# Ten and eleven seven-product pairs in the right half of the down projection, and a stretched second attention half

## The chip, the cores and the metric

The kernel runs on one core of a Trainium2 chip. The metric is the device time of one execution in microseconds (us). Time before: 2152.0 us, the median of three runs (2150.22, 2152.0 and 2154.43). The profile is that of one further execution.

## The reference

Two layers (`DEPTH = 2`) of a decoder trunk over 256 tokens of width 2048, all in float32:

```python
for l in range(DEPTH):
    h = _rmsnorm(x, attn_norm_g[l])
    proj = h @ w_in[l]                       # 2048 x 6144
    q, k, v, gate_b, gate_c, conv_in = jnp.split(proj, splits, axis=-1)
    ...                                      # QK-norm; differential attention, 8 heads; sub-layer norm
    conv = gate_b * _short_conv(gate_c * conv_in, conv_w[l])
    x = x + jnp.concatenate([attn, conv], axis=-1) @ w_out[l]       # 2048 x 2048
    hm = _rmsnorm(x, mlp_norm_g[l]) @ w_up[l]                       # 2048 x 8192
    x = x + jnp.square(jax.nn.relu(hm)) @ w_down[l]                 # 8192 x 2048
```

## The kernel before, in words

**Products.** Every weight and every activation is split into a high part (rounded to `fp32r` by ScalarE, e.g. L302) and a low part (the rest, by VectorE, e.g. L303). A product is three matmuls: high by high, high by low, low by high (`TERMS`). Weights come by DMA on SyncE's queue (SP) into raw tiles (four buffers), are split into `whi` and `wlo` (three buffers each, pool `wpool`) and used once. `Weights.take` hands out the next split tile and has those of up to three more jobs issued ahead.

**Order.** The order of TensorE (PE) is written out by the program (`manual_schedule`). The order on the other engines and on the DMA queues is worked out by the framework's scheduler from its own estimate of times, so it can move when anything else does. Attention, norms and the like are Python generators run beside the large products: `work.tick()` is called after each few matmuls, and a piece goes on after as many ticks as it last yielded.

**Mixer, per layer.** Six products q, k, v for heads 0 to 3, then for heads 4 to 7 (`linear`); then gc and ci four times in turn (`linear_t`, 64 matmuls and 16 ticks each, names gc00, ci00, gc01 ... in layer 0 and gc10 ... in layer 1), gb four times, and the output projection. Attention for heads 0 to 3 starts 3 ticks after the first v and runs beside q, k, v of the second half (`pace` 1). Attention for heads 4 to 7 starts 9 ticks into gc (`pace` 2). In `attention` each head is a `unit`: scores `sc` on PE, max and bias on VectorE (L610), exp on ScalarE (L619), weighting on VectorE (L622 to L630), then, 10 ticks later, transposes `ptp` on PE (L635), their split `pT` (L637, L638), and 4 ticks later the product with v, `av` (L646). `staggered` starts the four units 8 ticks apart. After the last unit the result is normed (L661 to L671), and after a further 12 (pace 1) or 18 ticks (pace 2) transposed, `atp`, and split into `cat` (L677 to L684). Beside gc and ci, VectorE also splits four weight tiles for each `linear_t`, joins its result (L422) and runs the short convolution (L772, L696), and GpSimd (POOL) multiplies by the norm's factors (L769, L700).

**MLP, per layer.** 32 pairs of 256 hidden columns. Of each pair the hidden values are computed (L949), squared, and multiplied by the left half of w_down (columns 0 to 1023) by seven products of blocks in place of eight (L992), as in Strassen's method; hidden values are also stored in DRAM, with the four sums that the seven products need where the pair is in `SEVEN` (`hid7`, L979), else without (`hid`, L984). Then the right half of w_down (columns 1024 to 2047) is taken with the stored hidden values. First the last two pairs (30 and 31), which are still on the chip. Then pairs 0 to `2 * BLK` - 1 one at a time: those in `SEVEN` by seven products (21 matmuls of 128x512), the others by `ordinary` (24). A pair of seven products needs its w_down rows split in other forms (`quarters`, L834 to L869: VectorE L840, L853, L856, L857; ScalarE L839) and its hidden values split after loading (L1099, L1100); an ordinary one has two `whi`/`wlo` tiles. Seven-product pairs gather four of their products in PSUM banks of their own (`prods` 1, 5, 6, 7), which `seven_onto(2)` adds onto x at the end (L1055, L1047, L1063: one ScalarE and eight VectorE instructions). Then the remaining pairs, two together as a block: `columns` takes block b for 512 columns at a time, 48 matmuls for a block's two halves, in the hand-written `order`. Of the hidden values, a pair's or block's tile `fb` comes from pool `apool` (four buffers, shared with the next layer's normed tiles nT), the first block's from `fpool`.

With `BLK = 12` pairs 0 to 23 are taken singly, nine of them by seven products, in both layers, and blocks 12, 13 and 14 follow in the order (12,0), (13,0), (12,1), (14,0), (13,1), (14,1).

**Between layers.** While the last blocks run in layer 0, the next layer's norm is made in four chunks (`norm.chunk`: eight transposes on PE (L454) into two PSUM banks, ScalarE L270 and VectorE L271 from there, squares on ScalarE L472). Chunks 0 and 1 need x's left half, chunks 2 and 3 the two column groups as they come out. Beside this, SP loads the first weights of the next stage: in the mixer, the four 1 MB tiles `uraw` that the MLP starts with (L809) follow in SP's queue once the attention's buffers are free.

Of the kernel before, what the change touches and what calls it, by code (L numbers as in the profile page):

```python
# [10 lines left out]
F32R = mybir.dt.float32r  # L11
# [4 lines left out]
P = 128  # L16
# [19 lines left out]
NB2 = DFF // (KG * P)  # L36


SEVEN = (2, 4, 7, 9, 12, 14, 17, 19, 22)
BLK = 12  # L40

TERMS = ((0, 0), (0, 1), (1, 0))
REL = 2 * S - P - 1
# [45 lines left out]
def staggered(pieces, apart):  # L89

    entries = [[i * apart, p] for i, p in enumerate(pieces)]
    while entries:
        for e in list(entries):
            if e[0] <= 0:
                try:
                    e[0] = max(1, next(e[1]))
                except StopIteration:
                    entries.remove(e)
                    continue
            e[0] -= 1  # L100
        if entries:
            yield 1
# [3 lines left out]
def trunk(ctx: ExitStack, tc: tile.TileContext, x, w_in, w_out, conv_w, q_norm_g, k_norm_g,  # L106
# [6 lines left out]
    apool = ctx.enter_context(tc.tile_pool(name="apool", bufs=4))  # L113
# [12 lines left out]
    def bank(name):  # L126
        return ps.tile([P, CH], F32, tag="bank", name=name)

    def wide(name):
        return nat.tile([P, CH], F32, tag="wide", name=name)  # L130

    work = Background()
# [292 lines left out]
    def rstd_of(ss, n, name, shape):  # L425

        e = small.tile([P, shape], F32, tag="rs_e", name=f"{name}_e")
        nc.gpsimd.tensor_scalar(e, ss, 1.0 / n, EPS, op0=ALU.mult, op1=ALU.add)
        r = small.tile([P, shape], F32, tag="rs_r", name=f"{name}_r")
        nc.gpsimd.tensor_tensor(r, e, mhalf[:, :shape], op=ALU.pow)  # L430
        return r
# [152 lines left out]
    def attention(l, qT, kT, kL, v, h0, dst, bias, tmp, pace):  # L584
# [9 lines left out]
        def unit(i):  # L594
# [31 lines left out]
            for t in range(NT):  # L626
# [2 lines left out]
                                               nlam[:, l:l + 1], op0=ALU.mult, op1=ALU.mult)  # L629
                nc.vector.scalar_tensor_tensor(p[:, w], s[:, 1, w], c[:, t:t + 1], s[:, 0, w],  # L630
                                               op0=ALU.mult, op1=ALU.add)
            yield 10
            tp = bank(f"ptp{h}")
            for b in range(3):
                nc.tensor.transpose(tp[:, b * P:(b + 1) * P], p[:, b * P:(b + 1) * P], ident)  # L635
            pT = tmp.tile([P, 2, 3 * P], F32R, tag="pT", name=f"pT{h}", bufs=1)
            nc.scalar.activation(pT[:, 0], tp[:, :3 * P], AF.Copy)  # L637
            nc.vector.tensor_sub(pT[:, 1], tp[:, :3 * P], pT[:, 0].bitcast(F32))  # L638
            yield 4

            av = ps.tile([P, CH], F32, tag="av", name=f"av{h}", bufs=1)
            av = av.rearrange("p (t n c) -> p t n c", t=NT, n=2)
# [19 lines left out]
            f = rstd_of(flat, P, f"a{h0}", 4 * NT)  # L662
# [3 lines left out]
            for t in range(NT):  # L666
# [3 lines left out]
                    ao[:, t].rearrange("p (g d) -> p g d", d=P),  # L670
                    f2[:, :, t:t + 1].to_broadcast([P, 4, P]), op=ALU.mult)  # L671
                an_.append(an)
            yield 12 if pace == 1 else 18
            for t in range(NT):
                tp = bank(f"atp{h0}_{t}")
                for b in range(4):
# [7 lines left out]
                    op0=ALU.mult, op1=ALU.subtract)  # L684
                yield 2

        yield from staggered([unit(i) for i in range(4)], 8)
        dst.ready = True

    def conv(l, q, u, cv, norm):  # L690
# [99 lines left out]
    def mlp(l, mnorm, last):  # L790

        norm = None if last else Norm(0, l + 1)
        mT = mnorm.tiles
        with ExitStack() as scope:
            upool = scope.enter_context(tc.tile_pool(name="upool", bufs=4))
            fpool = scope.enter_context(tc.tile_pool(name="fpool", bufs=2))
# [34 lines left out]
            def quarters(i, col=0):  # L831


                keep = late if i == 0 or (i == SEVEN[0] and col) else lambda ins: None  # L834

# [55 lines left out]
            for i in range(NP - LAG, NP):  # L891
# [5 lines left out]

            order = [(b - n, n) for b in range(BLK, NB2) for n in range(2)
                     if BLK <= b - n < NB2 - 1]

# [12 lines left out]
            def blocks_of(order):  # L913
                for b, n in order:
                    box = []
                    four(b, n, 0, box)
                    four(b, n, 2, box)

            blocks_of([(NB2 - 1, 0), (NB2 - 1, 1)])
            for i in range(2 * BLK):  # L920
                if i in SEVEN:
                    weights.jobs += quarters(i, 2 * CH)
                    continue
                box = []
                for k in range(2):
# [5 lines left out]
            hid = {i: dram.tile([P, 2, 4 * P], F32R, name=f"hid{l}p{i}")  # L931
                   for i in range(NP - LAG) if i not in SEVEN}
            hid7 = {i: dram.tile([P, 8 * P], F32, name=f"hid{l}s{i}") for i in SEVEN}

# [27 lines left out]
            def square(i, h):  # L962
# [9 lines left out]
                if i < NP - LAG:  # L972
# [4 lines left out]
                    nc.vector.tensor_sub(h[:, S4], h[:, A12], h[:, S2])  # L977
                if i in SEVEN:
                    nc.gpsimd.dma_start(hid7[i], h.rearrange("p a c -> p (a c)"))  # L979
# [16 lines left out]
            for i in range(NP):  # L996
                j = i - LAG
                end = i == NP - 1
# [13 lines left out]
                for c in range(2):  # L1012
# [15 lines left out]
                    if j >= 0 and c == 0:  # L1028
                        b11, b21, b22 = weights.take()
                        t1, t3 = weights.take()  # L1030
                        f = fs[j]
# [5 lines left out]
                    elif j >= 0:  # L1037
                        t2, t4 = weights.take()
                        f = fs[j]
# [6 lines left out]
            def onto(dst, p, base):  # L1046
                nc.vector.scalar_tensor_tensor(dst, p, mnorm.scale, base,  # L1047
                                               op0=ALU.mult, op1=ALU.add)

            def seven_onto(n):  # L1050


                x11, x21, x12, x22 = (xs[n + i][:, t] for i in range(2) for t in range(NT))
                e1, e2, e3, e4 = wide("e1"), wide("e2"), wide("e3"), wide("e4")
                nc.scalar.activation(e1, prods[1], AF.Copy, scale=mnorm.scale)  # L1055
                onto(e2, prods[6], e1)
                onto(e4, prods[5], e2)
                onto(x22, prods[5], x22)
                onto(e3, prods[7], e2)

                def add():
                    for dst, v in ((x11, e1), (x12, e4), (x21, e3), (x22, e3)):
                        nc.vector.tensor_add(dst, dst, v)  # L1063

                return add
# [23 lines left out]
            def pair(i, f=None, at=0):  # L1089

                if f is None:
                    f = apool.tile([P, 2, 8, P], F32R, tag="a", name="fb")
                if i not in SEVEN:
                    nc.gpsimd.dma_start(
                        f[:, :, at:at + 4].rearrange("p a k c -> p a (k c)"), hid[i])
                    return f
                back = fpool.tile([P, 8, P], F32, tag="h", name="back", bufs=1)
                nc.gpsimd.dma_start(back.rearrange("p a c -> p (a c)"), hid7[i])
                nc.scalar.activation(f[:, 0], back, AF.Copy)  # L1099
                nc.vector.tensor_sub(f[:, 1], back, f[:, 0].bitcast(F32))  # L1100
                return f

            def block(b):

                pool, tag = (fpool, "f") if b == BLK else (apool, "a")
                f = pool.tile([P, 2, 8, P], F32R, tag=tag, name="fb")
                for j in range(2):
                    pair(2 * b + j, f, 4 * j)
                return f
# [15 lines left out]
            def by_token(f, n):  # L1125

                parts = [weights.take() for _ in range(KG // 2)]
                for t in range(NT):
                    for k in range(KG):
                        for m, (pa, pw) in enumerate(TERMS):  # L1130
                            nc.tensor.matmul(  # L1131
                                accs[n][:, t], f(k, pa, t), parts[k // 2][pw][:, k % 2],
                                start=False, stop=(k == KG - 1 and m == 2))
                        work.tick()

            def columns(f, n, start=False, stop=False):

                for kp in range(KG // 2):
                    hi, lo = weights.take()
                    for k in (2 * kp, 2 * kp + 1):  # L1140
                        for t in range(NT):
                            for m, (pa, pw) in enumerate(TERMS):
                                nc.tensor.matmul(  # L1143
                                    accs[n][:, t], f(k, pa, t), (hi, lo)[pw][:, k % 2],
                                    start=(start and k == 0 and m == 0),
                                    stop=(stop and k == KG - 1 and m == 2))
                        work.tick()

            fs = {30: fs[30], 31: fs[31], 0: pair(0)}
            for n in range(2):  # L1150
                columns(lambda k, pa, t: fs[NP - LAG + k // 2][:, pa, k % 2 * 2 + t], n, start=True)
            for i in range(2 * BLK):
                if i + 1 < 2 * BLK:
                    fs[i + 1] = pair(i + 1)
# [5 lines left out]
                start, end = i == SEVEN[0], i == SEVEN[-1]  # L1160
# [11 lines left out]
                    if n == 5:  # L1172
                        work.tick()
                work.tick()
            seven_onto(2)()
            if not last:
                work.start(norm.chunk(0, 2), 6)
                work.start(norm.chunk(1, 2), 11)

            for b, n in order:  # L1180
                if n == 0 and b + 1 < NB2 - 1:
                    blocks[b + 1] = block(b + 1)
                units = lambda k, pa, t, f=blocks[b]: f[:, pa, 2 * k + t]
                if last and (b, n) == order[-1]:
                    by_token(units, n)
                else:
                    columns(units, n, stop=(b == NB2 - 2))
                if b == NB2 - 2:
                    for t in range(NT):
                        onto(xs[2 + n][:, t], accs[n][:, t], xs[2 + n][:, t])  # L1190
                    if last:
                        store(2 + n)
                    else:
                        work.start(norm.chunk(2 + n, 2))
        return norm

    norm = Norm(0, 0)
# [10 lines left out]
    for l in range(DEPTH):  # L1208
        mnorm = mixer(l, norm, first_loads if l == 0 else lambda weights: None)
        norm = mlp(l, mnorm, l == DEPTH - 1)  # L1210
# [31 lines left out]
```

## Time and profile before

| | |
|---|---|
| runs (us) | 2150.22, 2152.0, 2154.43 |
| the profiled execution | 2151.32 us, of which its span 2149.5 us |
| TensorE clock granted | 1.00 |
| PE | busy 2134.0 us, 10934 matmuls |
| VectorE (DVE) | busy 1678.6 us |
| ScalarE (ACT) | busy 1308.2 us |
| DMA | 475.98 MB, mean 221 GB/s |
| first and last 128x512 right-half product of layer 1 | from about 1982 to 2145 us |

A line of a group reads: source line, engine, operation, tile written <- tiles read, shape, count | busy time, mean of one | idle time of the engine just before it and what ended it. The mean of a matmul, about 390 ns for 128x512, is not what one costs in a row: matmuls overlap, and the next starts some 227 ns later. For what a matmul costs one reads the distance from start to start, or a run of them in the chain of waits.

### The profile page before, as it was taken

How to read it: one execution, taken by the hardware profiler on the slowest of the kernel's cores; microseconds unless marked ns; L12 is line 12 of the kernel's file. 1: busy time of each engine (PE TensorE's matmuls, PEld its weight loads, DVE VectorE, ACT ScalarE, POOL GpSimd, SP SyncE). 2: the span in 40 equal slices, each digit the busy share in tenths (PEclk: the TensorE clock that was granted, in tenths of full speed). 3: DMA queues.
4: the chain of work that ended last, by engine and by line, in shares of the span. 5: the costliest groups of instructions: out<-in, count | busy, mean ns of one | idle time of the engine just before them, and what ended most of it. 6: DMA issues, size and time to landing. Idle time of an engine off the chain costs nothing. (4 is left out here: it accounts for less than half of the span.)

```text
span 2149.5 us, 28983 instructions
## 1 busy us (share of the span) xinstructions
PE 2134.0 (99%) x10934; PEld 1819.9 (85%) x10934; DVE 1678.6 (78%) x2297; ACT 1308.2 (61%) x1767; POOL 169.8 (8%) x226
## 2 busy tenths in 40 slices
PE   9999999999999999999999999999999999999999
PEld 8888888888888888888888888888888888888887
DVE  6777655799889888798566776557888888888984
ACT  6666445666666666565566654446666666665652
POOL 3111100000000000011110111000000000001110
PEclk9999999999999999999999999999999999999999
DMA  8555766577777777798665566656777777777984
GB/s 271 179 160 171 246 186 187 190 244 230 233 232 231 229 227 234 241 318 288 210 178 176 166 197 215 187 176 204 241 233 223 240 229 226 235 225 262 335 264 137
DMA packets 298524, 475.98 MB, mean 221 GB/s; under 512 B 10803, under 2 KB 191621, under 8 KB 298384
## 3 DMA queue, kind: packets, MB, share of 16 engines
q1 hardware_dynamic: 268768, 406.88, 60.4%
q0 software_dynamic: 29568, 67.24, 9.4%
q8 instruction: 85, 1.39, 0.3%
q14 instruction: 55, 0.45, 0.1%
q10 hardware_dynamic: 48, 0.02, 0.0%
HBM read 440.52 MB, written 33.58 MB: 221 GB/s over the span
## 5 line engine op out<-in xcount | busy, mean ns | idle before, releaser
L303 DVE TENSOR_TENSOR wlo<-raw,whi 128x1024 fp32r<-128x1024 f32 x286 | 352.2, 1234 | 252.3 <-ACT whi L302 245.8
L302 ACT ACTIVATE whi<-raw 128x1024 fp32r<-128x1024 f32 x286 | 303.1, 1060 | 341.1 <-PE o L386 73.6
L949 PE MATMUL upc<-nT,uhi 128*128 128x512 f32 x1920 | 477.7, 391 | 0.6 <-ACT ev L959 0.6
L816 ACT ACTIVATE uhi<-uraw 128x1024 fp32r<-128x1024 f32 x256 | 271.2, 1060 | 280.3 <-PE upc L949 260.4
L949 PEld LDWEIGHTS upc<-nT,uhi 128*128 128x128 f32 x1920 | 352.7, 188 | 69.2 <-ACT ev L959 1.1
L817 DVE TENSOR_TENSOR ulo<-uraw,uhi 128x1024 fp32r<-128x1024 f32 x256 | 312.9, 1223 | 109.3 <-ACT uhi L816 105.3
L949 PEld LDWEIGHTS upc<-nT,ulo 128*128 128x128 f32 x1920 | 261.9, 190 | 18.7
L949 PE MATMUL upc<-nT,ulo 128*128 128x256 f32 x1920 | 267.7, 282 | 0.0
L386 PE MATMUL o<-whi,cat 128*128 128x512 f32 x512 | 159.5, 390 | 0.0
L1074 PE MATMUL dn<-whi,fb 128*128 128x512 f32 x480 | 151.1, 389 | 0.0
L386 PEld LDWEIGHTS o<-whi,cat 128*128 128x128 f32 x512 | 96.1, 188 | 19.7
L302 ACT ACTIVATE whi<-uraw 128x1024 fp32r<-128x1024 f32 x60 | 63.7, 1061 | 75.7 <-PE dn L1074 70.7
L1074 PEld LDWEIGHTS dn<-whi,fb 128*128 128x128 f32 x480 | 90.1, 188 | 18.7
L386 PE MATMUL o<-wlo,cat 128*128 128x512 f32 x256 | 99.6, 389 | 0.0
L840 DVE TENSOR_TENSOR t13l<-t,t13h 128x1024 fp32r<-128x1024 f32 x78 | 95.5, 1224 | 4.0 <-ACT t13h L839 2.2
L839 ACT ACTIVATE b2h<-draw 128x1024 fp32r<-128x1024 f32 x78 | 82.5, 1058 | 24.9 <-PE pr L992 22.2
L840 DVE TENSOR_TENSOR b2l<-draw,b2h 128x1024 fp32r<-128x1024 f32 x78 | 95.5, 1224 | 2.1 <-ACT b2h L839 2.1
L840 DVE TENSOR_TENSOR t24l<-t,t24h 128x1024 fp32r<-128x1024 f32 x78 | 95.2, 1221 | 1.4 <-ACT t24h L839 0.3
L853 DVE TENSOR_TENSOR t<-draw 128x1024 f32<-128x1024 f32 x78 | 95.3, 1221 | 0.4
L992 PE MATMUL pr<-t13h,f 128*128 128x512 f32 x240 | 93.8, 391 | 0.0
L1074 PE MATMUL dn<-wlo,fb 128*128 128x512 f32 x240 | 93.4, 389 | 0.0
L303 DVE TENSOR_TENSOR wlo<-uraw,whi 128x1024 fp32r<-128x1024 f32 x60 | 73.2, 1224 | 21.1 <-ACT whi L302 20.9
(408 smaller groups left out, 4138.6 us busy)
## 6 DMA issues: line engine op xcount, KB each, us to landing
uraw<-in_w_up_dram SPq DMA_DIRECT2D x128, 1024.0 KB, 6.5
raw<-in_w_in_dram SPq DMA_DIRECT2D x191, 512.0 KB, 4.0
draw<-in_w_down_dram SPq DMA_DIRECT2D x82, 1024.0 KB, 5.3
raw<-in_w_out_dram SPq DMA_DIRECT2D x64, 512.0 KB, 3.6
uraw<-in_w_down_dram SPq DMA_DIRECT2D x30, 1024.0 KB, 6.3
raw<-in_w_down_dram SPq DMA_DIRECT2D x16, 1024.0 KB, 5.2
hid0p<-f POOLq DMA_DIRECT2D x21, 512.0 KB, 6.4
fb<-hid0p POOLq DMA_DIRECT2D x21, 512.0 KB, 5.9
```

Of the source, the lines that this page charges most:

```text
L302: pair = (nc.scalar.activation(hi, raw, AF.Copy), nc.vector.tensor_sub(lo, raw, hi.bitcast(F32)))
L303: nc.vector.tensor_sub(lo, raw, hi.bitcast(F32)))
L386: nc.tensor.matmul(acc[:, t], a.ap[:, pa, k % KG, t * P:(t + 1) * P], (hi, lo)[pw][:, j], start=(k == 0 and n == 0), stop=(k == nk - 1 and ...
L816: pair = (nc.scalar.activation(hi, src, AF.Copy), nc.vector.tensor_sub(lo, src, hi.bitcast(F32)))
L817: nc.vector.tensor_sub(lo, src, hi.bitcast(F32)))
L839: keep(nc.scalar.activation(hi, src, AF.Copy))
L840: keep(nc.vector.tensor_sub(lo, src, hi.bitcast(F32)))
L853: keep(nc.vector.tensor_sub(t[:, 0:2], raw[:, :, 1], raw[:, 0]))
L949: nc.tensor.matmul(acc[:, 0] if part else acc, wt[:, k], a.ap[:, 0, k % KG] if part else a.ap[:, :, k % KG], start=(part == 0 and kh == 0 ...
L992: nc.tensor.matmul(prods[n], f[:, pa, a], b[pw], start=(start and m == 0), stop=(stop and m == 2))
L1074: nc.tensor.matmul(prods[p], f[:, pa, 2 * k + t], b[pw][:, n], start=(p in starts and k == 0 and m == 0), stop=(stop and k == 1 and m == 2))
```

## The change

`BLK` becomes 13 in layer 0 and 14 in layer 1, and the seven-product pairs are the entries of a longer list that lie below `2 * BLK`: layer 0 has pairs 0 to 25 singly, ten of them by seven products (24 is new), and then blocks 13 and 14; layer 1 has pairs 0 to 27 singly, eleven by seven products (24 and 27 are new), and then block 14 alone. `seven_onto(2)` is called right after the last pair of seven products: after pair 24 of 26 in layer 0, after pair 27 of 28 in layer 1. The first block's hidden values come from `apool` as the others do. In the attention every distance is multiplied by `pace`: for heads 4 to 7 the units start 16 ticks apart, `ptp` follows `sc` by 20 ticks, `av` follows `ptp` by 8, and `atp` follows by 24. The norm chunks in layer 0 start 4 and 8 ticks into the block stage, chunk 2 waits for 5 ticks after its columns, chunk 3 for 2 as before.

```diff
-SEVEN = (2, 4, 7, 9, 12, 14, 17, 19, 22)
-BLK = 12
+SEVEN_AT = (2, 4, 7, 9, 12, 14, 17, 19, 22, 24, 27)
+BLK_AT = (13, 14)
...
-            yield 10
+            yield 10 * pace
...
-            yield 4
+            yield 4 * pace
...
-            yield 12 if pace == 1 else 18
+            yield 12 * pace
...
-        yield from staggered([unit(i) for i in range(4)], 8)
+        yield from staggered([unit(i) for i in range(4)], 8 * pace)
...
     def mlp(l, mnorm, last):
 
         norm = None if last else Norm(0, l + 1)
+        BLK = BLK_AT[l]
+        SEVEN = [i for i in SEVEN_AT if i < 2 * BLK]
...
             def block(b):
 
-                pool, tag = (fpool, "f") if b == BLK else (apool, "a")
-                f = pool.tile([P, 2, 8, P], F32R, tag=tag, name="fb")
+                f = apool.tile([P, 2, 8, P], F32R, tag="a", name="fb")
...
                 work.tick()
-            seven_onto(2)()
+                if end:
+                    seven_onto(2)()
             if not last:
-                work.start(norm.chunk(0, 2), 6)
-                work.start(norm.chunk(1, 2), 11)
+                work.start(norm.chunk(0, 2), 4)
+                work.start(norm.chunk(1, 2), 8)
...
                     else:
-                        work.start(norm.chunk(2 + n, 2))
+                        work.start(norm.chunk(2 + n, (5, 2)[n]))
```

## The prediction

> **What bounds the kernel now.** I read the page's busy shares first, then the waits of PE alone, then the chain of waits and PE's timeline around each of those waits.
>
> ```profile
> span 2149.5 us, 28983 instructions
> ...
> PE 2134.0 (99%) x10934; PEld 1819.9 (85%) x10934; DVE 1678.6 (78%) x2297; ACT 1308.2 (61%) x1767; POOL 169.8 (8%) x226
> ```
>
> PE is busy nearly all the time, so only two things shorten the span: fewer matmuls, and the few us in which PE waits. The waits of PE, in full:
>
> ```profile
> PE pr L992 <- DVE f L982: 3.1, 2, 1.7
> PE ci L408 <- ACT whi L302: 1.9, 2, 1.6
> PE ptp L635 <- DVE s L630: 1.7, 2, 0.8
> PE sc L604 <- DVE cat L682: 1.2, 2, 0.6
> PE warm L160 <- DVE mhalf L152: 1.1, 1, 1.1
> PE av L648 <- DVE pT L638: 1.0, 2, 0.5
> PE upc L949 <- ACT ev L959: 0.6, 1, 0.6
> ```
>
> Columns: total us, times, longest. Four of the seven lines (sc, ptp, av, ci) are beside gc and ci, where attention for heads 4 to 7 runs, once per layer. The right half of the MLP has no line here. These times start where the previous matmul's modelled end is, which is too late; measured from start to start of consecutive matmuls the same waits are a little longer, and I use those.
>
> **Matmuls saved.** A run of 48 in the chain of waits gives the price of one:
>
> ```profile
> 2091.26 10.88 PE dn L1074 x48
> ...
> 2106.90 5.44 PE dn L1074 x24
> 2112.34 27.20 PE dn L1143 x120
> ```
>
> 10.88 / 48 = 0.2267 us. A seven-product pair has 21 where an ordinary one, or half a block, has 24. Before, both layers have 9 such pairs; after, 10 and 11. So 3 + 6 = 9 matmuls go: 9 x 0.2267 = **2.04 us**.
>
> What these three new pairs add elsewhere: VectorE's rows are 0.69 (b1l), 1.225 (b2l), 1.22 each for t, t13l, t24l, 0.69 twice (L856, L857) and 1.22 (L1100), together 8.2 us, against 2 x 1.225 = 2.45 us for an ordinary pair. Five pairs, two of them by seven products, then need 2 x 8.2 + 3 x 2.45 = 23.7 us of VectorE in 25.84 us of PE (2 x 4.76 + 3 x 5.44). Of two such stretches of 26 us:
>
> ```profile
> 2013.00:2039.00 26.00, 26.00 (x117) 21.52 (x116) 24.35 (x25) 16.24 (x18) 3.62 (x6) 1.00 0.95 332
> 2065.00:2091.00 26.00, 26.00 (x116) 21.52 (x115) 22.01 (x21) 14.26 (x15) 2.67 (x4) 1.00 0.80 262
> ```
>
> (busy us of PE, PEld, DVE, ACT, POOL; clock; DMA share; GB/s.) VectorE has 1.7 to 4 us to spare, and PE does not wait in nine such pairs per layer. The new ones keep two or three pairs' distance (22, 24, 27), so I cost their VectorE work at nothing. The cover is those 1.7 us; were it gone, each new pair would wait for about one low part, 1.22 us, 3.7 us for three. Their hidden values: 512 KB stored either way, landing in 2.9 us from h (hid1s) against 6.5 (hid1p); loads 7.2 against 6.4 us, issued about a pair (5 us) ahead as those of the other nine are. Nothing. The block whose tile moves to `apool` takes the buffer of a pair three before the last one; its two loads (6.4 us) have over 10 us.
>
> **Layer 1's end.** `seven_onto(2)` now runs with only block 14 to follow. From the row of pair 22: its VectorE chain starts 0.64 us before the last product ends (2106.26 against 2106.90) and takes 4.65 us (to 2110.91); then the low part of the last weight tile, 1.22 us, is ready 5.3 us after the product's end. PE needs it after 24 + 6 matmuls, 6.8 us. Nothing, with 1.5 us in hand; otherwise at most 1.2. The last stores follow the last matmul as before (2144.98 to 2149.5).
>
> **Layer 0's end.** The block stage has 16 ticks, not 24 (1.36 us each, 21.8 us). VectorE is idle 1.5 us in each 2.72 there (low parts at 1049.98 and 1052.70), 12 us in all; the addition (5.3), two chunks' splits of 1.95 us and x's third group (1.41) need 10.6. It fits, tightly. If not, the transposes wait for a bank, up to one chunk's splits, 1.95 us. A move forward brings nothing either: PE has no wait there now. Chunk 2's five ticks put it behind the last matmul that reads block 13's tile, whose buffer it takes. I take 0, range 0 to 2.
>
> **The attention's waits.** In PE's timeline of layer 0: `av` of the second unit is 0.62 late at 184.63; `ptp` of the third 0.18 late at 189.31; `ptp` of the fourth 0.96 late at 197.09 and 0.29 more inside it. Sum 2.05 us; layer 1 has the same four (0.62, 0.18, 0.96, 0.29 at 1251 to 1264), so 4.1 us in all. What is late: the fourth unit's scores start at 186.71 and its weighting is done at 197.0, a chain of 10.3 us through VectorE and ScalarE, in order behind weight splits and the previous unit; its distance of 10 ticks is 9.4 us of PE. At 20 ticks it is some 14.0 us of linear_t (11.17 us per 16 ticks) plus a unit's own matmuls, over 15 us. Likewise `pT` has 8 ticks, 5.6 us, where it was 0.62 us late at 2.8. VectorE's work per unit (about 3.4 us: 1.2 scores, 0.55 reciprocal and factors, 0.66 weighting, 0.5 pT, 0.4 ao) then lies beside a whole linear_t's (6.8 us), 10.2 us in 13.0 us of PE; before, it was 6.8 in 7.4. I take **-4.1 us**. PE's first `sc` wait (0.76 by start to start, twice) is on `cat` of the first half, and stays.
>
> A row that speaks against it: a copy of two numbers (L623) takes 0.86 us at 195.66, 0.17 elsewhere, while POOL's L700 runs (194.34 to 196.49); and a low part, 1.225 by its median, once took 2.316:
>
> ```profile
> L303 DVE TENSOR_TENSOR wlo<-raw,whi x286: 1203/1225/2316, 13.3 to 2137.9; 128x1024 fp32r<-128x1024 f32 x143
> ```
>
> So up to 1.1 us of VectorE go when POOL's multiplications fall on it. After the change, attention runs beside all of a layer's four gc/ci rounds, with two such POOL instructions each: at most 1.1 us more per unit, 11.3 of 13.0. It still fits. The Trainium skill has this as a rule (SBUF — State Buffer, Who interferes with whom): VectorE and GpSimd share a port pair, and whichever comes second waits for the other's whole instruction. By that rule a longer attention meets more of these; the sum would stand, with a smaller margin.
>
> **The wait on the prefetch.** Layer 1's chain:
>
> ```profile
> 1268.34 11.16 PE ci L408 x64
> ...
> 1281.48 10.49 DMA raw<-in_w_in_dram
> ...
> 1292.08 1.06 ACT whi L302
> ...
> 1293.18 7.02 PE ci L408 x37
> ```
>
> and SP's timeline:
>
> ```profile
> 1261.83 11.09 SPq L343 DMA_DIRECT2D raw<-in_w_in_dram  x4
> 1273.99 7.39 SPq L809 DMA_DIRECT2D uraw<-in_w_up_dram  x4
> 1281.48 18.54 SPq L343 DMA_DIRECT2D raw<-in_w_in_dram  x8
> ```
>
> When the attention's buffers come free, four 1 MB loads go out at once; the next raw tile (512 KB) is behind them in SP's queue for 7.4 us and lands 18.0 us after the burst's start. PE needs it 16.2 us after and waits 1.78 us (0.49 in layer 0, 16.7 after the burst, at 207.54). In the changed order SP has three of the loads, a raw tile, then the fourth, and this after 30 of the 48 gc/ci/gb raw tiles, not 20. 3.67 of 4.72 MB bring the first raw tile at 13.0 to 14.0 us. It is needed later, too: the burst comes about 9 ticks behind the last `av` (6 us before), which is now at tick 85 and was at 47; tile 30 is used at tick 120, tile 20 was at 80: 26 ticks against 24, some 1.4 us more, 17.6 us at least. The second tile, at 20 us, has 20.4. I take both waits as gone: **-2.26 us**; the other end is 0, and a wait of 1 us on the second tile lies between. The Trainium skill (DMA: Bandwidth & Descriptors, Queues, rings and completion order) says that each DMA engine takes one row's descriptors in ring order; so the burst's bytes ahead of a tile count and not only its place in time, which is the scaling used; without it both waits would stay.
>
> **Sum.** -2.04 - 4.1 - 2.26 = -8.4 us. The profiled execution took 2151.32 us, so 2142.9; it lies 0.7 below the median of the runs, 2152.0, within their spread of -1.8 to +2.4. Against the median: **2143.6 us**. The MLP's own starts (pr L992, upc L949: DMA of draw tiles, 3.7 us of waits) are not touched.
>
> **Rivals.**
> (a) The burst hits again. It moves to a place where the same kind of raw tile comes, and 3 MB are still ahead of it. Then -6.1: 2145.9. Against it: the nearly two ticks and the megabyte gained.
> (b) The attention's waits move, not go: the scheduler has reordered VectorE's queue, and a stretched unit meets other splits. The nearest row is the present wait per unit; if as much comes back at ci and gb, only the matmuls are left: 2150.0. Against it: at pace 1 the first half of attention runs at the short distances beside `linear` with VectorE less loaded, and PE's list has no wait from it.
> (c) Slower: SP's queue is in order, and the first `uraw` there waits for the attention's last read. All raw tiles behind wait too. If that read comes X us later than the place chosen for it, tile 30 lands X after the 13.5 us above and has 17.6; PE waits X - 4.1 in each layer. The total passes +4.3 (0.2%) where 2(X - 4.1) - 6.1 > 4.3, X > 9.3. One linear_t with its unit, 13.0 us, gives 2 x 8.9 - 6.1 = +11.7: 2163.7. For it: the wait of SP on that place is there now, 1.0 us long, and it doesn't depend on PE alone. Against it: PE fixes the last `av` in ticks, and from there it is POOL's 3 us and two VectorE instructions.
>
> **Chances.** A run's median of this kernel tells about 0.2%, 4.3 us, from no change. Forecast 0.70 (own range 2141 to 2146.5, from the runs' spread and the small bounds above); (a) 0.10; (b) 0.12; (c) 0.08. Faster 0.80, same 0.12, slower 0.08. The range takes in (a) and (b)'s end and, downwards, the runs' spread: 2140.5 to 2150.0.
>
> **What would show it.** PE's instructions fall by 9 matmuls to 10925. In the waits of PE the lines av <- pT, ptp <- s and ci <- whi are gone, sc <- cat and pr stay. In SP's timeline three `uraw` issues, a raw one, and a fourth, with the raw tile landing within 14 us. No line of dn L1143 or L1074 appears. Wrong would be: a wait of PE on wlo or tpn at the layers' ends, on whi in ci03/gb0 (rival a or c), or ptp and av lines of the old size (b).

## The result, and the profile after

The changed kernel takes 2141.7 us (median of five runs, 2140.61 to 2142.45), against 2152.0 before (five runs, 2150.22 to 2154.43): a ratio of 0.9951, 95% interval 0.9939 to 0.9962. It is faster, by 10.3 us in the medians; 2143.6 was predicted, a gain of 8.4. The profiled execution of the changed kernel took 2141.7 us, its span 2139.9, 9.6 us below the span before.

The head of the page after, and PE's list of waits (total us, times, longest):

```profile
span 2139.9 us, 28980 instructions
...
PE 2129.0 (99%) x10925; PEld 1817.0 (85%) x10925; DVE 1699.2 (79%) x2315; ACT 1316.2 (62%) x1776; POOL 164.3 (8%) x226
```

```profile
PE pr L994 <- DVE f L984: 3.2, 2, 1.7
PE sc L604 <- DVE cat L682: 1.2, 2, 0.6
PE warm L160 <- DVE mhalf L152: 1.1, 1, 1.1
PE upc L951 <- ACT ev L961: 0.8, 1, 0.8
```

There are nine matmuls fewer, and the lines av, ptp and ci are gone; sc, pr and the start of the MLP stand as they were. To see where the time went, I cut PE's timeline at the first matmul of each stage and take the distances (us):

| stage | layer 0 before | after | layer 1 before | after |
|---|---|---|---|---|
| first q to first gc | 147.71 | 147.65 | 144.07 | 143.95 |
| first gc to first gb (attention of heads 4 to 7) | 102.87 | 99.79 | 104.19 | 100.05 |
| gb and the output projection | 134.44 | 134.44 | 134.44 | 134.44 |
| first up to first dn of the right half | 514.07 | 514.13 | 515.23 | 515.39 |
| right half, to the next q or the last matmul | 171.01 | 170.34 | 168.49 | 167.12 |

The second row gives 3.08 + 4.14 = 7.2 us, the last 0.67 + 1.37 = 2.04. The remaining 0.4 us is the start before the first q (8.48 and 8.11), which varies from 7.7 to 8.8 between executions of any of these kernels.

The right half: VectorE's timeline at the end of layer 1, from the last product of pair 27:

```profile
2123.89 1.54 DVE L1049 SCALAR_TENSOR_TENSOR e<-pr1r,rowf,e 128x512 f32<-128x512 f32 x2 [1.16 <-PE pr1r L994]
...
2126.66 1.89 DVE L1065 TENSOR_TENSOR x<-x,e 128x512 f32<-128x512 f32 x3
2128.46 1.22 DVE L303 TENSOR_TENSOR wlo<-raw,whi 128x1024 fp32r<-128x1024 f32 x1
```

The chain of additions holds up the last low part until 2129.68. PE's first matmul after the last product starts at 2124.37, so this is 5.3 us, and PE needs it 6.8 us after, 30 matmuls on. It doesn't wait.

The prefetch, in layer 1: SP's timeline, ScalarE's, and the chain of waits over the same stretch.

```profile
1295.25 3.68 SPq L811 DMA_DIRECT2D uraw<-in_w_up_dram  x3
1299.03 3.23 SPq L343 DMA_DIRECT2D raw<-in_w_in_dram  x1
1302.31 1.23 SPq L811 DMA_DIRECT2D uraw<-in_w_up_dram  x1
```

```profile
1310.44 1.06 ACT L302 ACTIVATE whi<-raw 128x1024 fp32r<-128x1024 f32 x1 [2.53 <-DMA raw<-in_w_in_dram]
1314.45 1.06 ACT L302 ACTIVATE whi<-raw 128x1024 fp32r<-128x1024 f32 x1 [2.94 <-DMA raw<-in_w_in_dram]
```

```profile
1307.18 8.37 PE ci L408 x48
1315.56 0.00 issue
1315.56 3.06 PE ci L408 x16
```

Three loads, a raw tile, a fourth load, as foretold. ScalarE starts on a tile when it has landed: 15.2 us after the burst for the first, 19.2 for the second. From there it is 1.06 us to the split tile, 1315.51, and PE wants the second at 1315.4: from start to start it loses 0.27 us there, too little for the list. It is that close. ("Landed" is below, too, where ScalarE starts on the tile, about 0.1 us after the last byte.)

### The profile page after: what moved, and what is told of

Same layout as the page of the kernel before. It is cut to its first block, busy times and chain, and to the rows that moved or that the text cites. A ratio compares the mean times of both kernels' runs of the same rounds, so it can differ in the third digit from the quotient of the medians.

```text
span 2139.9 us, 28980 instructions
## 1 busy us (share of the span) xinstructions
PE 2129.0 (99%) x10925; PEld 1817.0 (85%) x10925; DVE 1699.2 (79%) x2315; ACT 1316.2 (62%) x1776; POOL 164.3 (8%) x226
## 4 chain that ended last, share of the span: by engine, by line
PE 97%; DVE 1%; ACT 1%; DMA 1%; issue 0%; DVEq 0%; ACTq 0%
PE upc L951 31%; PE pr L994 13%; PE dn L1076 8%; PE o L386 8%; PE ci L408 4%; PE gb L408 4%; PE q L386 4%; PE k L386 4%; PE v L386 4%; PE gc L408 4%; PE dn L994 2%; PE dn L1144 2%; PE pr1r L994 1%; PE pr0r L994 1%; PE upw L951 1%; PE up L951 1%
## 5 line engine op out<-in xcount | busy, mean ns | idle before, releaser
L303 DVE TENSOR_TENSOR wlo<-raw,whi 128x1024 fp32r<-128x1024 f32 x274 | 341.7, 1248 | 221.1 <-ACT whi L302 219.6
L302 ACT ACTIVATE whi<-raw 128x1024 fp32r<-128x1024 f32 x274 | 290.4, 1060 | 306.8 <-PE o L386 73.6
L951 PEld LDWEIGHTS upc<-nT,ulo 128*128 128x128 f32 x1920 | 261.9, 190 | 18.7
L1076 PE MATMUL dn<-whi,fb 128*128 128x512 f32 x528 | 166.1, 389 | 0.0
L302 ACT ACTIVATE whi<-uraw 128x1024 fp32r<-128x1024 f32 x66 | 70.0, 1061 | 84.0 <-PE dn L1076 79.0
L1076 PEld LDWEIGHTS dn<-whi,fb 128*128 128x128 f32 x528 | 99.1, 188 | 20.6
L1076 PE MATMUL dn<-wlo,fb 128*128 128x512 f32 x264 | 102.7, 389 | 0.0
L303 DVE TENSOR_TENSOR wlo<-uraw,whi 128x1024 fp32r<-128x1024 f32 x66 | 80.5, 1222 | 19.7 <-ACT whi L302 19.5
```

The costliest lines, as they stand in the source:

```text
L302: pair = (nc.scalar.activation(hi, raw, AF.Copy), nc.vector.tensor_sub(lo, raw, hi.bitcast(F32)))
L303: nc.vector.tensor_sub(lo, raw, hi.bitcast(F32)))
L951: nc.tensor.matmul(acc[:, 0] if part else acc, wt[:, k], a.ap[:, 0, k % KG] if part else a.ap[:, :, k % KG], start=(part == 0 and kh == 0 ...
L1076: nc.tensor.matmul(prods[p], f[:, pa, 2 * k + t], b[pw][:, n], start=(p in starts and k == 0 and m == 0), stop=(stop and k == 1 and m == 2))
```

## The experiments

Each ratio is to the kernel before, run beside the experiment: its median was 2151.7 us in experiments 1 to 4, 2153.0 in 5 to 8 and 2152.2 in 9 and 10. Times of different groups are therefore not set against each other; what a part of the change is worth is read from the stages of the profiles.

"Floor" below is a stage from gc to gb without any of the waits discussed, 98.99 us; with the first `sc` wait, which was not to change, 99.73.

**1. The attention's four distances alone, on the kernel before.**

```diff
-            yield 10
+            yield 10 * pace
...
-            yield 4
+            yield 4 * pace
...
-            yield 12 if pace == 1 else 18
+            yield 12 * pace
...
-        yield from staggered([unit(i) for i in range(4)], 8)
+        yield from staggered([unit(i) for i in range(4)], 8 * pace)
```

> The kernel before with the attention's distances doubled and nothing else. Theory (three separate terms that add up): 2.0 us of the changed kernel's gain is matmuls, the rest is PE's waits beside gc and ci, so the span falls by 7.2 us here (the stage from the first gc to the first gb went from 102.9 to 99.8 us in layer 0 and from 104.2 to 100.1 in layer 1 in the changed kernel), to about 2142.3, and the lines av, ptp and ci leave PE's waits. Rival (the longer stretch of pairs and its earlier chunks also free PE by way of the scheduler's order, or the distances need them): less than 5 us here.

Measured: 2143.88 us (five runs, 2142.76 to 2145.11), ratio 0.9965 (0.9952 to 0.9977). From gc to gb 99.77 and 99.87 us, that is -7.4 in all; the right half as before. PE's waits are those of the changed kernel.

**2. The seven-product pairs alone**: the changed kernel with the four distances of the kernel before.

```diff
-            yield 10 * pace
+            yield 10
...
-        yield from staggered([unit(i) for i in range(4)], 8 * pace)
+        yield from staggered([unit(i) for i in range(4)], 8)
```

> The changed kernel with the attention's distances as before. Theory: 9 matmuls fewer at 0.227 us, so the span falls by 2.0 us, to about 2147.5, all of it from the first dn on; av, ptp and ci stay in PE's waits at their sizes of before. Rival (the three new pairs of seven products, the tighter block stage or the addition just before the last block cost PE something that the attention's gain hid): less than 1 us of gain, and a wait on wlo, nT or a bank after the first dn.

Measured: 2148.4 us (eleven runs, 2145.53 to 2150.83), ratio 0.9985 (0.9976 to 0.9994). The right half lost 0.65 and 1.37 us, 2.02 in all. PE's waits in the mixer:

```profile
PE ci L408 <- ACT whi L302: 1.8, 2, 1.2
PE ptp L635 <- DVE s L630: 1.7, 2, 0.9
PE sc L604 <- DVE cat L682: 1.2, 2, 0.6
...
PE av L648 <- DVE pT L638: 1.0, 2, 0.5
```

They are those of before, though the ci wait is shared out otherwise: 0.9 us more in layer 0, 1.05 less in layer 1, with the same order of loads. So in the profiles 1 and 2 add up: -7.4 and -2.02 are the -9.3 of the change, within 0.2. In the medians experiment 2 gains 3.3 us, more than its 2.0 of matmuls; its runs spread over 5.3 us, and the interval, 1.3 to 5.2 us, takes in both.

**3. Only the spacing of the units.** The prediction gave a reason for the waits of ptp and av: a chain of 10.3 us that is longer than its distance. If that is so, spacing alone, with the old 10 and 4 ticks, should leave them.

```diff
-        yield from staggered([unit(i) for i in range(4)], 8)
+        yield from staggered([unit(i) for i in range(4)], 8 * pace)
```

> The kernel before with only the units of the second attention half 16 ticks apart instead of 8; within a unit ptp still follows sc by 10 ticks and av follows ptp by 4. Theory of latency (the prediction's: the chain from scores to weighting, 10.3 us, is longer than its distance, 9.4 us): ptp stays late by some 0.5 to 1 us and av by some 0.5 in each layer, three to four times, so 2 to 4 us of the 4.1 stay. Rival, load (the chain is only so long because two units and the weight splits stand in VectorE's and ScalarE's queues together): with units apart the same distance is enough, av and ptp go from PE's waits and the span falls by some 6 to 7 us, as with everything doubled.

Measured: 2147.5 us (one run), span 2145.7. PE's waits in the mixer:

```profile
PE gc L408 <- ACT whi L302: 2.6, 4, 1.1
...
PE sc L604 <- DVE cat L682: 1.2, 2, 0.6
```

No ptp and no av: the reason fell. A unit of layer 0 in PE's timeline (scores, then the transposes they wait for) and in VectorE's (its last weighting):

```profile
190.49 0.39 PE L604 MATMUL sc<-kT,qT 128*128 128x128 f32 x2
...
198.39 0.49 PE L635 MATMUL ptp<-ident,s 128*128 128x128 f32 x3
```

```profile
195.99 0.74 DVE L630 SCALAR_TENSOR_TENSOR s<-s,c 128x128 f32<-128x128 f32 x2
```

The chain from scores to weighting takes 6.2 us here (190.49 to 196.73), not 10.3, and the distance of 10 ticks, now 7.9 us, is ample. The kernel before could have shown it. The first and the fourth unit there, from PE's and VectorE's timelines:

```profile
163.56 0.22 PE L604 MATMUL sc<-kT,qT 128*128 128x128 f32 x1
...
186.71 0.39 PE L604 MATMUL sc<-kT,qT 128*128 128x128 f32 x2
```

```profile
169.91 0.74 DVE L630 SCALAR_TENSOR_TENSOR s<-s,c 128x128 f32<-128x128 f32 x2
...
196.69 0.74 DVE L630 SCALAR_TENSOR_TENSOR s<-s,c 128x128 f32<-128x128 f32 x2
```

The first unit, with none of the other three in the queues, takes 7.1 us to the last of its two weightings, 0.8 of them PE's wait for `cat`; the fourth takes 10.7 (10.3 to the first of the two). In these 10.7 us VectorE is busy without a gap, in the 6.2 of experiment 3 for 5.4. What made 10.3 us of it was the work of the units before it in VectorE's and ScalarE's queues: load, not latency. (In the third unit's 10.8 us VectorE is busy for 7.9, so the order in the queues counts beside the amount of work; no run separates the two.)

In place of these waits stands the burst's. SP has the changed kernel's order (three loads, a raw tile, a fourth), and PE still waits, on the second tile more than on the first:

```profile
231.85 10.53 DMA raw<-in_w_in_dram
...
242.49 1.06 ACT whi L302
...
243.60 3.06 PE gc L408 x16
```

The burst went out at 223.37, and the first tile landed 15.0 us after it (238.37), as in the changed kernel (14.7 and 15.2). But the burst lies 26 raw tiles into the stage, not 30, and PE wants the two tiles 15.7 and 19.0 us after it. In the changed kernel that is 17.4 and 20.1 us. So the megabyte that is no longer ahead doesn't end the wait by itself. Nor does the time of the need: in the kernel before, too, PE wanted its first tile behind the burst at 17.4 us (its matmuls started 17.9 and 19.2 us after the burst, 0.5 and 1.8 late), and behind four loads that tile landed at 16.8 and 18.1. The changed kernel has both, three loads ahead and 17.4 us.

**4. The burst taken apart**, on the kernel before: a copy of one column of x (group 0 for the first two buffers, group 1 for the next two) into each of the first four buffers makes their loads, and those behind them, wait for the output projection. The column is overwritten by the load.

```diff
+                        if i < 2:
+                            nc.vector.tensor_copy(raws[kh][:, 0, 0:1], xs[i][:, 0, 0:1])
                         nc.sync.dma_start(
```

> The kernel before; the first four 1 MB tiles of the MLP's up weights are held back by a one-column copy from x's groups 0 and 1 (overwritten by the load), so that they go out two at a time beside the output projection and not as a burst beside gc and ci. Theory: the waits of PE on whi at ci (0.49 and 1.78 us) go and av and ptp stay: the span falls by 2.3 us, to about 2147.3, if the pairs of loads cost nothing beside o. Rival (the wait at ci is VectorE's and ScalarE's backlog from the attention, the DMA only the last to be named): ci stays in PE's waits.

Measured: 2148.67 us (one run), span 2146.9; from gc to gb 102.28 and 102.31, that is -0.59 and -1.88. PE's waits there, without sc:

```profile
PE ptp L635 <- DVE s L630: 1.7, 2, 0.9
...
PE av L648 <- DVE pT L638: 1.0, 2, 0.5
```

The ci line is gone and nothing else: the prefetch is worth 2.5 us, and the term is its own. What is left above 99.73 is the attention's part, 2.55 and 2.58 us.

**5. Spacing and late loads together**, experiments 3 and 4 in one.

> The kernel before with the second half's units 16 ticks apart (all other distances as before) and the first four up-weight tiles held back as in the run with the late loads. Theory after the first four runs: the spacing alone ends the waits of av and ptp, and the further distances in a unit did no more than move the burst of loads by two ticks against the raw tiles; so with the burst out of the way the stage from gc to gb takes 99.8 us in each layer as with everything doubled, and the span falls by 7.2 to 7.5 us from 2149.5. Rival (the longer distances in a unit save PE something of their own): the stage stays above 100.5 us with no wait on whi named.

Measured: 2145.14 us (one run), span 2142.6, 6.9 us below the span before; 99.73 us from gc to gb in both layers, the floor with the sc wait. So the doubled spacing is enough for all of the attention's part, and the doubled distances within a unit only move the burst to where it hurts less (76.8 us after the first gc in place of 67.3). Those distances at the old spacing weren't tried, so whether they would have done as well stays open: `s` has two buffers, so what a unit takes must fit in twice the spacing.

**6. The second half starts later**, at 12 ticks of gc rather than 9, in the changed kernel, against its first sc wait.

```diff
-1 + half), 3 + 6 * half)
+1 + half), 3 + 9 * half)
```

> The changed kernel with the second attention half started 12 ticks into gc in place of 9. Theory: the wait that is left there, sc on cat (0.77 us by start to start in each layer), is a PSUM bank that VectorE frees about 0.8 us late; three ticks, 2 us, end it, and the span falls by 1.5 us to about 2138.4, if the burst of loads, which moves by the three ticks too, does not fall worse against the raw tiles. Rival: the burst's place decides; a wait on whi at ci or gb of 0.3 to 1.8 us per layer takes the gain.

Measured: 2140.06 us (five runs, 2139.32 to 2141.8), ratio 0.9943 (0.993 to 0.9955). The sc line is gone, but the burst's wait is back in layer 1, 0.84 us. The burst didn't move by three ticks, as expected: it went out 76.4 us after the first gc, against 76.8 in the changed kernel, though the last `av` came 1.1 us later.

**7. Later start and late loads**, the changed kernel with 4 and 6.

> The changed kernel with the later start (12 ticks) and the first four up-weight tiles held back until beside the output projection, two at a time. Theory: the sc waits (2 x 0.77) and the last wait on whi (0.27 in layer 1) are gone, no burst meets gc and ci: the span falls by 1.8 us against the changed kernel, to about 2138.1. Rival: the held-back loads come with their own wait beside o or at the MLP's start: same as the changed kernel or slower.

Measured: 2139.76 us (five runs, 2139.24 to 2140.42), ratio 0.9941 (0.9928 to 0.9953); 98.99 us from gc to gb in both layers. PE's waits, in full:

```profile
PE pr L996 <- DVE f L986: 3.1, 2, 1.7
PE warm L160 <- DVE mhalf L152: 1.1, 1, 1.1
```

**8. Every second pair by seven products**, in the changed kernel: 12 and 13 pairs. This takes away the room on VectorE by which the three new pairs were costed at nothing.

```diff
-SEVEN_AT = (2, 4, 7, 9, 12, 14, 17, 19, 22, 24, 27)
+SEVEN_AT = tuple(range(2, 28, 2))
```

> The changed kernel with every second pair of the right half by seven products (2, 4, 6 ... 24 or 26): 12 and 13 in place of 10 and 11, 12 matmuls fewer. Theory (VectorE is the cover, 8.2 us for such a pair and 2.45 for an ordinary one, against 4.76 and 5.44 of PE): two pairs need 10.65 us of VectorE in 10.20 of PE, so PE waits 0.45 us per two pairs once the lead of some 2 us is used up, 3.5 to 4 us in each layer, on wlo, b2l, t13l or t24l; less 1.36 us of matmuls in each layer: the span rises by 4 to 5 us, to about 2144.5. Rival (VectorE is no bound there, its busy share only follows PE): the span falls by 2.7 us.

Measured: 2144.11 us (five runs, 2140.05 to 2147.11), ratio 0.9959 (0.9946 to 0.9973). New lines among PE's waits:

```profile
PE pr0r L994 <- DVE t24l L842: 0.8, 2, 0.6
PE pr1r L994 <- DVE t24l L842: 0.6, 1, 0.6
PE pr0r L994 <- DVE t13l L842: 0.3, 1, 0.3
PE pr1r L994 <- DVE t13l L842: 0.2, 1, 0.2
```

Two pairs more per layer save 6 matmuls, 1.36 us, so the right half should have come to 168.98 and 165.76 us. It took 171.00 and 167.43: waits of 2.0 and 1.7 us, more than was saved. It is half of what I expected, but on the low parts that the theory names. (The runs spread over 7 us, so the cost is read from the profile.) In this profile the burst also cost 1.2 and 1.4 us (100.93 and 101.13 from gc to gb, over 99.73), though nothing was changed there.

**9 and 10. The changed kernel and that of experiment 7 once more**, side by side on one chip.

> The changed kernel once more, beside the next one on the same chip. The burst's wait (whi at ci) differs between profiles of kernels with the same mixer: 0.27 us in the changed kernel, 0 with the attention alone, 2.2 with the dense pairs. If that is chance in the loads' landing, this profile shows a wait between 0 and 2.3 us there and the same waits as before elsewhere, and a median within 1.5 us of 2141.7.

> The changed kernel with the later start and the held-back loads once more, on the same chip as the changed kernel. Theory: no wait at gc, ci or gb in any execution, so it is 1.8 to 3 us faster than the changed kernel; rival: within 0.5 us of it.

Measured: 2141.97 us (five runs, 2141.28 to 2144.37; ratio 0.9952, 0.9939 to 0.9966) and 2139.44 us (2139.0 to 2141.05; 0.994, 0.9928 to 0.9953). The runs do not overlap: later start and late loads are worth 2.5 us in the medians, and this version beats both kernels.

Both profiles show something that the first ones of these two kernels didn't. In the changed kernel's second execution the burst's wait is back; its chain in layer 1, where the burst went out at 1295.38:

```profile
1304.72 10.97 DMA raw<-in_w_in_dram
...
1315.80 1.06 ACT whi L302
...
1316.91 3.08 PE ci L408 x16
```

The second tile landed after 20.4 us, not 19.2, and from gc to gb the two layers took 0.6 and 1.5 us over the 99.73. And the late loads are no safe place either: in layer 0 of the other kernel, two of them ahead of the output projection's weights cost PE 1.6 us (91.38 us from o to up in place of 89.75), once in the eight layers profiled with late loads.

```profile
PE o L386 <- DVE wlo L303: 0.8, 1, 0.8
PE o L386 <- ACT whi L302: 0.3, 1, 0.3
```

## Why the prediction was right, and where it was not

The time lies in the forecast's own range, 2141 to 2146.5, and the gain came from the three terms named. One by one:

- **Matmuls saved, -2.04.** Right to the hundredth: -2.04 in the change, -2.02 alone (experiment 2).
- **VectorE's work for the new pairs, 0.** Right, for the reason given: PE waits on nothing there, and where the spacing of the sevens is tightened to every second pair it waits on the low parts at once (experiment 8). The price of a lost cover, one low part (1.22 us) for each pair too many, was of the right kind: four pairs too many cost 3.7 us. The limit lies between 11 sevens in 28 pairs and 13.
- **The ends of both layers, 0.** Right. In layer 1 the last low part is ready 5.3 us after the product, exactly as worked out. In layer 0 the range up to 2 was not needed: the right half there fell by the 0.67 us of its three matmuls.
- **The attention's waits, -4.1.** The size was a little small: 5.1 us by experiments 4 and 5. The waits ended, but not for the reason given. The step that failed is "a chain of 10.3 us ... its distance of 10 ticks is 9.4 us of PE. At 20 ticks it is ... over 15 us", which takes the chain's length as given and lengthens the distance. With units 16 ticks apart the chain itself falls to 6.2 us, and the old distance is enough (experiments 3 and 5). Nearer was the step beside it, VectorE's work per unit against the time that it lies in: VectorE was busy for all of the fourth unit's chain. I had both, and could have told them apart from the trace of before, where the first unit takes 7.1 us. The wrong one made no difference here, but it kept longer distances within a unit that the attention's waits did not need.
- **Small steps, not in the sum.** The stage fell by 7.2 us, and the terms give 4.1 + 2.26 - 0.27 = 6.1. The other 1.1 went, for the most part, in steps of some 50 to 105 ns between matmuls beside the attention's, of which PE's list of waits shows none. Comparing a stage's length with its floor finds them.
- **The wait on the prefetch, -2.26.** Nearly right in the profile (0.27 left) and right as a mechanism (experiment 4: -2.5), but with less room than I said, for two steps failed. The first is "needed later ... some 1.4 us more, 17.6 us at least". There the need is that of the landed tile, 16.2 us before, which with the split behind it is PE's 17.4; and 17.4 it still was. The tile's need did move 1.4 us further from the last `av` (23.8 to 25.2 us), but the burst came 7.9 us behind that `av`, not 6.4 as before, and this took the 1.4. The second is the landing "at 13.0 to 14.0 us": it was 14.7 and 15.2, and 15.4 and 16.3 in the second execution. So what ended the wait is the one load less ahead of the tile: 2.1 and 2.9 us earlier than behind four (16.8 and 18.1), where "3.67 of 4.72 MB" gave 3.7 to 4.0. By the Trainium skill (DMA: Bandwidth & Descriptors, Queues, rings and completion order) each DMA engine takes a row's descriptors in ring order. The trace agrees in that fewer bytes ahead bring the tile sooner, though by less than their share. The second tile, "at 20 us, has 20.4", had 19.0 for want of the same 1.4, and landed at 18.7 and 19.2. That the profile lost only 0.27 us there is in part luck: which way it falls changes from one execution to the next, and in the other profile it was about 2. Experiment 10's gain of 2.5 us over the changed kernel, of which 1.5 are its two sc waits, puts about 1 us on the burst in an average run.
- **The port shared with POOL.** The row that spoke against the change was real, and its size bounded well. The group of VectorE's low parts (minimum, median and maximum in ns):

```profile
L303 DVE TENSOR_TENSOR wlo<-raw,whi x274: 1201/1225/2183, 12.8 to 2128.5; 128x1024 fp32r<-128x1024 f32 x137
```

Ten low parts took over 1.3 us, against four before, each beside one of POOL's multiplications (L700, L769); the longest lost 0.96 us where 1.1 was allowed. No wait of PE followed. By the Trainium skill (SBUF — State Buffer, Who interferes with whom) the port pair that VectorE shares with GpSimd is an exclusive lock. The trace agrees: beside POOL's work the low parts took up to 2.18 us, and a longer stretch met more of it.

- **The rivals.** (a), the burst hits again, was the right one to fear: not in the profile of the changed kernel, but in its second execution, and in experiments 3, 6 and 8. (b) and (c) didn't come: no wait moved to gc, ci or gb other than the burst's, and SP's first load came 1.5 us later behind the last `av` than before, where (c) needed more than 4.1 for a wait.

## What to carry to other kernels

A long chain between two instructions of one engine is not yet a latency. Look whether the pieces in it wait for each other's data or stand in a queue behind another instance's; in the second case more distance between instances is what helps, and more distance within one only needs buffers. And a tile whose landing and need lie within a microsecond is a wait in some executions: measure both from the burst, since what moves the need may move the burst with it, and look at a second profile before the term is called gone.

## What the runs showed of the hardware

With several 1 MB loads outstanding, SP's own issuing slows: an issue takes 0.37 us by its median, and the three loads of the burst took 3.68 us together, the raw tile behind them 3.23 us alone. A 512 KB tile lands in 4.0 us by its median. Counted from the start of a burst of 1 MB loads ahead of it, it took 16.8 to 18.1 us behind four (the kernel before and experiment 2) and 14.1 to 16.3 behind three (the changed kernel and experiments 1, 3, 6, 8 and 9), differing by 1.1 us between two executions of the same kernel; behind two it took 11.5 to 12.5 us in seven layers, and 14.9 in the one where the late loads hurt.
